# Head norm of the mLSTM inside its output stage, per head and 512 tokens, with the split state in one buffer

## The chip, the cores and the metric

The kernel runs on one core of one Trainium2 chip. The metric is the device time of one execution in microseconds (us), as the median of several runs. Engines are named as the profile names them: PE is TensorE, DVE is VectorE, ACT is ScalarE, POOL is GpSimd, and SP is SyncE, whose queue issues nearly all DMAs.

## What is computed

One encoder layer over two sequences of 1,024 ("prompt") and 2,048 tokens ("sample"), each with 16 learned tokens in front. A single input projection (1,024 to 6,672 columns) feeds two branches: a 2-D neighbourhood attention and a bidirectional mLSTM with four heads of 128. Both go through a final stage with two gates and an output projection. The change is in the end of the mLSTM branch:

```python
h = (h_f + h_b)[:, :, P:].transpose(0, 2, 1, 3)
h = sigmoid(o_pre).reshape(B, L, ML_HEADS, ML_HEAD_DIM) * h
mu = mean(h, axis=-1); var = mean(square(h - mu), axis=-1)
h = (h - mu) * rsqrt(var + EPS)
yb_in = h.reshape(B, L, ML_WIDTH) * head_g          # per-channel gain
yb = (yb_in * silu(ml_z)) @ w_b
```

So each token's 128 values of each head are gated, brought to mean 0 and variance 1, and multiplied by a gain and by a second gate.

## The kernel before

All large products are made in three: an fp32 operand is split into a high and a low part (`xh`/`xl`, `whi`/`wlo`, `cch`/`ccl` and so on), and high x high, high x low and low x high are added in PSUM (`mm3`, L141).

TensorE's order is written by hand; a scheduler orders the instructions of the other engines and the DMAs on SP. TensorE's order comes from two generators. `dense` makes the input projection in groups of 1,024 tokens and, for every 512 tokens, a final block (`final`, `("f", s, b)` in `PLAN`). `sparse` makes, after each other, mLSTM of the prompt, attention of the prompt, mLSTM of the sample, attention of the sample. `run` (L1453) interleaves them: whenever `sparse` yields a cost (`A_A` for a piece of mLSTM outputs, `A_N` for a piece of the norm, in us), `dense` goes on until it has issued that much of its own products. A larger cost therefore puts more dense products between two pieces.

`ml(s)` (L863) works in three stages. For each head `ml_states` goes over the blocks of 256 tokens from the end and keeps the states; `ml_outputs` (L990) goes forward, block by block. One block `b` of `ml_outputs` has six pieces, with a `yield A_A` after each: scores of `b`; first half of the products of `p = b - 1` (`back(p, 0)`); loads; second half (`back(p, 1)`); splits and `finish(p)`; `state(b + 1)`. `state` (L1050) copies the state of a block into its high and low part `cch`, `ccl`, in two buffers, one block ahead of use; `kv` (L1030) does the same for v (`vh`, `vl`). `finish` (L1101) divides by the denominator and stores the block of h, 256 tokens x 128, into the DRAM tensor `H`.

When all heads are done, `ml_norm` (L1158) reads `H` back in blocks of 128 tokens x 4 heads (`hn`), with the gates `tog` (from `TO`) and `szg` (from `SZ`). For each two blocks VectorE gates, takes mean and variance (`bn_stats`, `bn_aggr`) and an inverse root in eleven small steps (`rsqrt8`, L125); then it normalises and multiplies by `szg`; TensorE transposes (L1207), ScalarE evicts into `ybo`, and four stores go to `YB`. The pieces of the norm cost `A_N` each. The gain `head_g` is multiplied into `SZ` already when it is made (`tm_store`, L438).

After `ml_norm` of the prompt, `na(0, ...)` (L554) begins: its first loads, `qr` and `kr` (L552), lead to the first scores (L668).

Of the kernel before, what the change touches and what calls it, by code (L numbers as in the profile page):

```python
# [9 lines left out]
F32 = mybir.dt.float32  # L10
# [97 lines left out]
A_NA, A_D, A_A, A_N, A_G = 1.12, 1.63, 1.63, 1.85, 1.3  # L108


class K:
# [55 lines left out]
    def setup2(self):  # L167
# [10 lines left out]
        nc.vector.tensor_scalar(self.cw[:, 12:24], self.cw[:, 12:24], S_K, None, op0=ALU.mult)  # L178
        self.ones = cp.tile([P, P], F32, name="ones")
# [9 lines left out]
        self.H = [t(f"h{s}", [SEQLEN[s], 512]) for s in range(2)]  # L189
# [197 lines left out]
    def tm_unit(self, col, halves, wd):  # L387
# [4 lines left out]
        if C_MZ <= col < C_MO:  # L392
            hg = wp.tile([P, 1, 256], F32, name="hgb", bufs=1)
            nc.sync.dma_start(hg[:, 0, :], _bc(self.i["head_g"], col - C_MZ, wd))
            nc.vector.tensor_scalar(hg, hg, -0.125, None, op0=ALU.mult)
            self.hgt = hg
# [29 lines left out]
    def tm_store(self, col, wd, s, n, cnt, tok, st):  # L426
# [6 lines left out]
        if C_MZ <= col < C_MO:  # L433
# [3 lines left out]
            for a in range(2):  # L437
                nc.vector.tensor_tensor(st[:, a, :wd], st[:, a, :wd], self.hgt[:, 0, :], op=ALU.mult)  # L438
# [551 lines left out]
    def ml_outputs(self, mp, s, h, g, NB, sts):  # L990
# [3 lines left out]
        raws, kfs, vas, ums, convs, qs, kss, vs, shs, cs, nums = ({} for _ in range(11))  # L994

        def load(b):
            if b < NB:
# [32 lines left out]
        def kv(b):  # L1030
            if b < NB:
                kf, va = kfs.pop(b), vas.pop(b)
# [4 lines left out]
                vh = mp.tile([P, CB, 130], F32R, name="vh", bufs=2)  # L1037
                vl = mp.tile([P, CB, 130], F32R, name="vl", bufs=2)
                nc.scalar.activation(f2(vh), f2(va), AF.Copy)
                nc.vector.tensor_tensor(f2(vl), f2(va), f2(vh).bitcast(F32), op=ALU.subtract)  # L1040
                kss[b], vs[b] = (kh, kl), (vh, vl)
# [8 lines left out]
        def state(b):  # L1050

            if b < NB:
                for j in range(CB):
# [5 lines left out]
                cch = mp.tile([P, CB, 260], F32R, name="cch", bufs=2)  # L1059
                ccl = mp.tile([P, CB, 260], F32R, name="ccl", bufs=2)  # L1060
# [22 lines left out]
        def back(b, j):  # L1083
# [12 lines left out]
            if j == 0:  # L1096
                nums[b] = mp.tile([P, CB, 2, 130], F32, name="num", bufs=1)
            num = nums[b]
            nc.vector.tensor_tensor(num[:, j].rearrange("p d c -> p (d c)"), pa[:, :260], tt.rearrange("p d c -> p (d c)"), op=ALU.add)

        def finish(b):  # L1101
# [8 lines left out]
            hb = mp.tile([P, CB, P], F32, name="hb", bufs=2)  # L1110
            for j in range(CB):
                nc.scalar.activation(hb[:, j], num[:, j, 0, 0:P], AF.Copy, scale=den[:, j, 0:1])
                nc.vector.scalar_tensor_tensor(hb[:, j], num[:, j, 1, 0:P], den[:, j, 1:2], hb[:, j], op0=ALU.mult, op1=ALU.add)
            nc.sync.dma_start(self.H[s][t0:t0 + BL, h * P:(h + 1) * P].rearrange("(c p) f -> p c f", p=P), hb)
# [14 lines left out]
        state(0)  # L1129
        yield A_A  # L1130
        for b in range(NB + 1):
            p = b - 1
            if b < NB:
                scores(b)
                conv_a(b + 1)
# [19 lines left out]
            state(b + 1)  # L1155
            yield A_A

    def ml_norm(self, mp, s):  # L1158

        nc = self.nc  # L1160
        N = SEQLEN[s] // (2 * P)
        ld, hs, rr = {}, {}, {}

        def load(i):
            if i < N:
                ld[i] = []
                for e in range(2):
                    rows = slice((2 * i + e) * P, (2 * i + e + 1) * P)
                    hb = mp.tile([P, 4, P], F32, name="hn", bufs=6)
                    to = mp.tile([P, 4, P], F32, name="tog", bufs=4)  # L1170
                    sz = mp.tile([P, 4, P], F32, name="szg", bufs=4)
                    for x, dr in ((hb, self.H), (to, self.TO), (sz, self.SZ)):
                        nc.sync.dma_start(x.rearrange("p a b -> p (a b)"), dr[s][rows, :])
                    ld[i].append((hb, to, sz))

        def stats(i):
            bs = mp.tile([P, 2, 4, 6], F32, name="bs", bufs=2)
            mv = mp.tile([P, 2, 4, 2], F32, name="mv", bufs=2)
            for e in range(2):
                hb, to, _ = ld[i][e]  # L1180
                nc.vector.scalar_tensor_tensor(hb, to, 1.0, hb, op0=ALU.add, op1=ALU.mult)
                for h in range(4):
                    nc.vector.bn_stats(bs[:, e, h], hb[:, h])
                for h in range(4):
                    nc.vector.bn_aggr(mv[:, e, h], bs[:, e, h])
                yield A_N
            ve = mp.tile([P, 2, 4], F32, name="ve", bufs=2)
            nc.vector.tensor_scalar(ve, mv[:, :, :, 1], 4.0 * EPS, None, op0=ALU.add)
            rr[i] = mv, self.rsqrt8(mp, ve, [P, 2, 4])

        def norm(i, e):
            mv, r = rr[i]
            hb, _, sz = ld[i][e]
            for h in range(4):
                nc.vector.tensor_scalar(hb[:, h], hb[:, h], mv[:, e, h, 0:1], r[:, e, h:h + 1], op0=ALU.subtract, op1=ALU.mult)
            nc.vector.tensor_tensor(hb, hb, sz, op=ALU.mult)

        def turn(i, e):
            if i < 0:
                return  # L1200
            hb = ld[i][e][0]
            if e == 0:
                rr[i] = mp.tile([P, 4, 2, P], F32, name="ybo", bufs=2)
            yo = rr[i]
            pt = self.psum("tr", [P, 4, P])
            for h in range(4):
                nc.tensor.transpose(pt[:, h, :], hb[:, h], self.ident)  # L1207
            nc.scalar.activation(yo[:, :, e, :], pt, AF.Copy)
            if e:
                for h in range(4):  # L1210
                    nc.sync.dma_start(self.YB[s][h][:, 2 * P * i:2 * P * (i + 1)], yo[:, h].rearrange("p a b -> p (a b)"))
                ld.pop(i)
                rr.pop(i)

        load(0)
        yield A_N
        for i in range(N + 1):
            if i < N:
                load(i + 1)
                yield from stats(i)  # L1220
                yield A_N
            turn(i - 1, 0)
            if i < N:
                norm(i, 0)
            yield A_N
            turn(i - 1, 1)
            if i < N:
                norm(i, 1)
            yield A_N
        self.done.add(("ml", s))  # L1230
# [283 lines left out]
```

## Time and profile before

| | us |
|---|---|
| median of 3 runs | 2914.11 |
| lowest and highest | 2910.47, 2915.75 |
| the profiled execution itself | 2923.43 |
| its span in the profile | 2921.6 |
| PE busy in the span | 2818.3 |
| DVE busy | 1742.9 |
| ACT busy | 1289.8 |

The profile shows one execution. Busy time is the time in which at least one instruction of the engine runs; matmuls overlap, so that a busy PE still need not be at its fastest. Idle time stands behind the last bar of a group's line, with what ended most of it. `PEclk` is the share of TensorE's full clock that was granted. A stage is read best from busy time in a window (start and end in us from the span's beginning).

### The profile page before, as it was taken

The numbers are of one execution on the slowest core, as the hardware profiler recorded it, in microseconds if no ns is written. First come the engines' busy times: TensorE is split into PE (matmuls) and PEld (weight loads), VectorE is DVE, ScalarE is ACT, GpSimd is POOL, SyncE is SP. The second block draws the span as 40 slices with busy tenths as digits, with TensorE's granted clock in tenths as the row PEclk, the third lists the DMA queues.
The fourth block names the chain that finished last, engine by engine and source line by source line (L and its number), as shares of the span: only waits on it lengthen the run. The fifth ranks groups of instructions, "written<-read, shape, count | busy, mean of one in ns | idle before, by whom it ended". The sixth has DMA issues, their size and how long they took to land.

```text
span 2921.6 us, 49506 instructions
## 1 busy us (share of the span) xinstructions
PE 2818.3 (96%) x17488; PEld 2511.0 (86%) x17488; DVE 1742.9 (60%) x4722; ACT 1289.8 (44%) x3114; POOL 23.2 (1%) x107
## 2 busy tenths in 40 slices
PE   6999999999799999999999999999999999989998
PEld 6998897899689988788887988888888888879887
DVE  5233566556656665466568776565555557777853
ACT  4112555543244444356566554513444445545421
POOL 1000000000000000000000000000000000000000
PEclk9999999999999999999999999999999999999999
DMA  9655676755875654478679898568669659887975
GB/s 351 220 175 185 201 219 216 270 180 172 294 222 160 205 168 144 143 242 297 202 232 347 279 328 284 157 233 275 199 183 291 206 163 273 249 284 250 295 258 196
DMA packets 438760, 675.26 MB, mean 231 GB/s; under 512 B 52240, under 2 KB 253024, under 8 KB 438512
## 3 DMA queue, kind: packets, MB, share of 16 engines
q1 hardware_dynamic: 437392, 669.41, 70.2%
q0 software_dynamic: 1120, 2.69, 0.4%
q8 instruction: 138, 2.26, 0.3%
q14 instruction: 110, 0.90, 0.1%
HBM read 455.05 MB, written 216.90 MB: 230 GB/s over the span
## 4 chain that ended last, share of the span: by engine, by line
PE 80%; DMA 9%; DVE 7%; issue 2%; ACT 1%; SPq 1%; DVEq 0%; ACTq 0%
PE pj L144 13%; PE pj L145 13%; PE pj L146 13%; PE pj L412 6%; PE pj L413 6%; PE pj L414 6%; PE pj L1326 3%; PE pj L1328 3%; PE pj L1327 3%; PE sm L705 3%; PE tr L693 2%; DMA tg<-gt 2%; DMA um<-ud 1%; PE sc L668 1%; PE sc L669 1%
## 5 line engine op out<-in xcount | busy, mean ns | idle before, releaser
L144 PE MATMUL pj<-xh,whi 128*128 128x512 f32 (+1 forms) x1824 | 720.0, 395 | 0.0
L145 PE MATMUL pj<-xl,whi 128*128 128x512 f32 (+1 forms) x1824 | 702.6, 385 | 0.1
L146 PE MATMUL pj<-xh,wlo 128*128 128x512 f32 (+1 forms) x1824 | 700.9, 384 | 0.0
L412 PE MATMUL pj<-whi,xh 128*128 128x256 f32 (+3 forms) x1576 | 450.0, 286 | 0.0
L413 PE MATMUL pj<-wlo,xh 128*128 128x256 f32 (+3 forms) x1576 | 443.9, 282 | 0.0
L414 PE MATMUL pj<-whi,xl 128*128 128x256 f32 (+3 forms) x1576 | 443.5, 281 | 0.0
L146 PEld LDWEIGHTS pj<-xh,wlo 128*128 128x128 f32 x1824 | 345.4, 189 | 72.3
L144 PEld LDWEIGHTS pj<-xh,whi 128*128 128x128 f32 x1824 | 345.7, 190 | 56.6
L145 PEld LDWEIGHTS pj<-xl,whi 128*128 128x128 f32 x1824 | 346.2, 190 | 54.9 <-DVE xl L310 0.4
L412 PEld LDWEIGHTS pj<-whi,xh 128*128 128x128 f32 (+1 forms) x1576 | 293.5, 186 | 1.2
L413 PEld LDWEIGHTS pj<-wlo,xh 128*128 128x128 f32 (+1 forms) x1576 | 293.2, 186 | 1.1
L414 PEld LDWEIGHTS pj<-whi,xl 128*128 128x128 f32 (+1 forms) x1576 | 293.3, 186 | 0.9
L676 ACT ACTIVATE prb<-sc,mx 128x384 f32<-128x384 f32 (+2 forms) x192 | 120.1, 626 | 237.3 <-DVE mx L672 229.6
L1326 PE MATMUL pj<-whi,mh 128*128 128x256 f32 x768 | 221.1, 288 | 1.1 <-ACT mh L1308 0.7
L1328 PE MATMUL pj<-whi,mlo 128*128 128x256 f32 x768 | 217.7, 284 | 1.8 <-DVE mlo L1309 1.8
L1327 PE MATMUL pj<-wlo,mh 128*128 128x256 f32 x768 | 217.6, 283 | 0.0
L696 DVE TENSOR_TENSOR pts<-tr,pts 96x512 fp32r<-96x512 f32 (+2 forms) x192 | 132.0, 687 | 117.2 <-ACT pts L695 115.9
L421 DVE TENSOR_TENSOR stT<-pj,bb 128x256 f32<-128x256 f32 (+3 forms) x197 | 83.3, 423 | 151.2 <-PE pj L414 147.1
L144 PE MATMUL pj<-yh,whi 128*128 128x512 f32 x384 | 157.4, 410 | 9.3 <-DVE tg L1305 9.3
L695 ACT ACTIVATE pts<-tr 96x512 fp32r<-96x512 f32 (+2 forms) x192 | 114.1, 594 | 115.9 <-PE tr L693 115.6
L672 DVE CUSTOM_DVE_ANT_1 sc<-sc,gt 128x384 f32<-128x384 f32 (+2 forms) x192 | 118.6, 618 | 74.5 <-PE sc L669 62.6
L145 PE MATMUL pj<-yl,whi 128*128 128x512 f32 x384 | 152.8, 398 | 0.0
(234 smaller groups left out, 5069.4 us busy)
## 6 DMA issues: line engine op xcount, KB each, us to landing
whi<-wh SPq DMA_DIRECT2D x176, 512.0 KB
wlo<-wl SPq DMA_DIRECT2D x176, 512.0 KB
wh<-whi SPq DMA_DIRECT2D x64, 512.0 KB
wl<-wlo SPq DMA_DIRECT2D x64, 512.0 KB
wraw<-w_in SPq DMA_DIRECT2D x48, 512.0 KB
gt<-st SPq DMA_DIRECT2D x96, 256.0 KB
tg<-gt SPq DMA_DIRECT2D x96, 256.0 KB
xh<-xh SPq DMA_DIRECT2D x6, 2048.0 KB
```

What stands on the lines that cost most here:

```text
L144: mm(out, ah, bh, start=start, stop=False)
L145: mm(out, ah, bl, start=False, stop=False)
L146: mm(out, al, bh, start=False, stop=stop)
L412: nc.tensor.matmul(o, xh, wh, start=k == 0, stop=False)
L413: nc.tensor.matmul(o, xh, wl, start=False, stop=False)
L414: nc.tensor.matmul(o, xl, wh, start=False, stop=k == KT - 1)
L672: nc.vector.tensor_tensor_reduce(out=so, in0=so, in1=gt[:, g0:g0 + ns, c0:c0 + 32], op0=ALU.add, op1=ALU.min, scale=-1.0, scalar=3.0e38, a ...
L676: nc.scalar.activation(pr_[:, :N].rearrange("p (b a c) -> p b a c", b=4, c=8), sc[:, :N].rearrange("p (a b c) -> p b a c", b=4, c=8), AF.E ...
L696: nc.vector.tensor_tensor(pts[:ks, :, 1, :], pt[:ks], pts[:ks, :, 0, :].bitcast(F32), op=ALU.subtract)
L1326: nc.tensor.matmul(o, mh[:, k, xs], wh, start=k == 0, stop=False)
L1327: nc.tensor.matmul(o, mh[:, k, xs], wl, start=False, stop=False)
L1328: nc.tensor.matmul(o, ml[:, k, xs], wh, start=False, stop=k == KT - 1)
```

## The change

The norm of one head and 512 tokens becomes a generator of its own, `ml_norm(mp, s, h, q, hb, tz)`, made by `finish` when two blocks of `hb` are ready, and stepped by `ml`: one step after each piece of `ml_outputs` and of the next head's `ml_states`. Its first step gates and takes the statistics, the second makes the inverse root, the third normalises and multiplies by `szg`; eight steps later come the four transposes, ScalarE's eviction in place, now with the gain as a scale for each partition, and one store to `YB`. h stays in SBUF; `H` is gone. The gates are loaded by `gates(p)` as 512 tokens x 128 columns. `vh`, `vl`, `cch` and `ccl` have one buffer each; `state(b)` makes all four, at the end of block `b`'s pieces, just before the next block's. `num` takes the place of `tt`. `A_A` is 1.87 instead of 1.63.

```diff
-A_NA, A_D, A_A, A_N, A_G = 1.12, 1.63, 1.63, 1.85, 1.3
+A_NA, A_D, A_A, A_G = 1.12, 1.63, 1.87, 1.3
...
+        self.hg = cp.tile([P, 4], F32, name="hg")
+        nc.sync.dma_start(self.hg, i["head_g"].rearrange("(h p) -> p h", p=P))
+        nc.vector.tensor_scalar(self.hg, self.hg, -0.125, None, op0=ALU.mult)
...
-        self.H = [t(f"h{s}", [SEQLEN[s], 512]) for s in range(2)]
...
-            for a in range(2):
-                nc.vector.tensor_tensor(st[:, a, :wd], st[:, a, :wd], self.hgt[:, 0, :], op=ALU.mult)
...
+                norm = iter(())
                 for h in range(4):
                     sts = {}
-                    yield from self.ml_states(mp, s, h, g, NB, sts)
-                    yield from self.ml_outputs(mp, s, h, g, NB, sts)
-        with tc.tile_pool(name=f"mn{s}", bufs=1, side="right", reuse_waits="tile") as mp:
-            yield from self.ml_norm(mp, s)
+                    for cost in self.ml_states(mp, s, h, g, NB, sts):
+                        next(norm, None)
+                        yield cost
+                    norms = deque()
+                    for cost in self.ml_outputs(mp, s, h, g, NB, sts, norms):
+                        if next(norm, "end") == "end" and norms:
+                            norm = norms.popleft()
+                        yield cost
+                    if norms:
+                        for _ in norm:
+                            pass
+                        norm = norms.popleft()
+                for _ in norm:
+                    yield A_A
+        self.done.add(("ml", s))
...
+        def gates(b):
+            if b % 2:
+                tzs[b // 2] = [mp.tile([P, 4, P], F32, name=n, tag="tz", bufs=2) for n in ("tog", "szg")]
+                for x, d in zip(tzs[b // 2], (self.TO, self.SZ)):
+                    nc.sync.dma_start(x, d[s][(b - 1) * BL:(b + 1) * BL, h * P:(h + 1) * P].rearrange("(c p) f -> p c f", p=P))
...
-                vh = mp.tile([P, CB, 130], F32R, name="vh", bufs=2)
-                vl = mp.tile([P, CB, 130], F32R, name="vl", bufs=2)
-                nc.scalar.activation(f2(vh), f2(va), AF.Copy)
-                nc.vector.tensor_tensor(f2(vl), f2(va), f2(vh).bitcast(F32), op=ALU.subtract)
...
         def state(b):
             if b < NB:
+                va = vas.pop(b)
+                vh = mp.tile([P, CB, 130], F32R, name="vh", bufs=1)
+                vl = mp.tile([P, CB, 130], F32R, name="vl", bufs=1)
+                nc.scalar.activation(f2(vh), f2(va), AF.Copy)
+                nc.vector.tensor_tensor(f2(vl), f2(va), f2(vh).bitcast(F32), op=ALU.subtract)
...
-                cch = mp.tile([P, CB, 260], F32R, name="cch", bufs=2)
-                ccl = mp.tile([P, CB, 260], F32R, name="ccl", bufs=2)
+                cch = mp.tile([P, CB, 260], F32R, name="cch", bufs=1)
+                ccl = mp.tile([P, CB, 260], F32R, name="ccl", bufs=1)
...
-            tt = mp.tile([P, 2, 130], F32, name="tt", bufs=1)
+            if j == 0:
+                nums[b] = mp.tile([P, CB, 2, 130], F32, name="num", bufs=1)
+            num = nums[b]
             for d in range(2):
-                nc.scalar.activation(tt[:, d], pi[:, 130 * d:130 * d + 130], AF.Copy, scale=g[d]["e"][:, cc, h:h + 1])
+                nc.scalar.activation(num[:, j, d], pi[:, 130 * d:130 * d + 130], AF.Copy, scale=g[d]["e"][:, cc, h:h + 1])
...
-            nc.sync.dma_start(self.H[s][t0:t0 + BL, h * P:(h + 1) * P].rearrange("(c p) f -> p c f", p=P), hb)
+            if a:
+                norms.append(self.ml_norm(mp, s, h, q, hbs.pop(q), tzs.pop(q)))
...
-        state(0)
         yield A_A
         for b in range(NB + 1):
             p = b - 1
+            if p >= 0:
+                gates(p)
...
-            state(b + 1)
+            state(b)
...
-    def ml_norm(self, mp, s):
...
+    def ml_norm(self, mp, s, h, q, hb, tz):
+        nc = self.nc
+        to, sz = tz
+        nc.vector.scalar_tensor_tensor(hb, to, 1.0, hb, op0=ALU.add, op1=ALU.mult)
+        bs = mp.tile([P, 4, 6], F32, name="bs", bufs=1)
+        mv = mp.tile([P, 4, 2], F32, name="mv", bufs=1)
+        for j in range(4):
+            nc.vector.bn_stats(bs[:, j], hb[:, j])
+        for j in range(4):
+            nc.vector.bn_aggr(mv[:, j], bs[:, j])
+        yield
+        nc.vector.tensor_scalar(mv[:, :, 1], mv[:, :, 1], 4.0 * EPS, None, op0=ALU.add)
+        rs = self.rsqrt8(mp, mv[:, :, 1], [P, 4])
+        yield
+        for j in range(4):
+            nc.vector.tensor_scalar(hb[:, j], hb[:, j], mv[:, j, 0:1], rs[:, j:j + 1], op0=ALU.subtract, op1=ALU.mult)
+        nc.vector.tensor_tensor(hb, hb, sz, op=ALU.mult)
+        for _ in range(8):
+            yield
+        pt = self.psum("tr", [P, 4, P])
+        for j in range(4):
+            nc.tensor.transpose(pt[:, j, :], hb[:, j], self.ident)
+        nc.scalar.activation(hb, pt, AF.Copy, scale=self.hg[:, h:h + 1])
+        nc.sync.dma_start(self.YB[s][h][:, 512 * q:512 * q + 512], hb.rearrange("p a b -> p (a b)"))
```

More of the change, by code (lines that the diff above doesn't have):

```diff
@@ L391, in tm_unit @@
         nc.sync.dma_start(bb[:, :wd], _bc(self.i["b_in"], col, wd))
[L392 to L396, printed above, removed]
         todo = []
@@ L988, in ml_states, with ml_outputs @@
             yield A_D
-    def ml_outputs(self, mp, s, h, g, NB, sts):
+    def ml_outputs(self, mp, s, h, g, NB, sts, norms):
         nc = self.nc
         f2 = lambda x: x.rearrange("p c t -> p (c t)")
-        raws, kfs, vas, ums, convs, qs, kss, vs, shs, cs, nums = ({} for _ in range(11))
+        raws, kfs, vas, ums, convs, qs, kss, vs, shs, cs, nums, tzs, hbs = ({} for _ in range(13))
         def load(b):
@@ L1031, in kv @@
             if b < NB:
-                kf, va = kfs.pop(b), vas.pop(b)
+                kf = kfs.pop(b)
                 kh = mp.tile([P, CB, P], F32R, name="kh", tag="kh", bufs=2)
@@ L1052, in state @@
             if b < NB:
+                va = vas.pop(b)
[3 more added lines that the diff above has]
+                nc.vector.tensor_tensor(f2(vl), f2(va), f2(vh).bitcast(F32), op=ALU.subtract)
+                vs[b] = vh, vl
                 for j in range(CB):
@@ L1095, in back @@
                 self.mm3(pa[:, 130 * d:130 * d + 130], sh[:, d, j, :], sl[:, d, j, :], vh[:, j, :], vl[:, j, :])
[L1096 to L1099, printed above, removed]
+            nj = num[:, j].rearrange("p d c -> p (d c)")
+            nc.vector.tensor_tensor(nj, pa[:, :260], nj, op=ALU.add)
         def finish(b):
@@ L1109, in finish @@
             nc.vector.reciprocal(den, den)
-            hb = mp.tile([P, CB, P], F32, name="hb", bufs=2)
+            q, a = b // 2, CB * (b % 2)
+            if not a:
+                hbs[q] = mp.tile([P, 2 * CB, P], F32, name="hb", bufs=2)
+            hb = hbs[q]
             for j in range(CB):
-                nc.scalar.activation(hb[:, j], num[:, j, 0, 0:P], AF.Copy, scale=den[:, j, 0:1])
-                nc.vector.scalar_tensor_tensor(hb[:, j], num[:, j, 1, 0:P], den[:, j, 1:2], hb[:, j], op0=ALU.mult, op1=ALU.add)
-            nc.sync.dma_start(self.H[s][t0:t0 + BL, h * P:(h + 1) * P].rearrange("(c p) f -> p c f", p=P), hb)
+                o = hb[:, a + j]
+                nc.scalar.activation(o, num[:, j, 0, 0:P], AF.Copy, scale=den[:, j, 0:1])
+                nc.vector.scalar_tensor_tensor(o, num[:, j, 1, 0:P], den[:, j, 1:2], o, op0=ALU.mult, op1=ALU.add)
+            if a:
+                norms.append(self.ml_norm(mp, s, h, q, hbs.pop(q), tzs.pop(q)))
             for x in (shs, vs, qs, ums):
@@ L1154, in ml_outputs @@
             decay(b + 1, 1)
-            state(b + 1)
+            state(b)
             yield A_A
-    def ml_norm(self, mp, s):
+    def ml_norm(self, mp, s, h, q, hb, tz):
         nc = self.nc
[L1161 to L1230, printed above, removed]
```

2 lines of the change are left out of this document (1 added, 1 removed).

## Prediction, made before the changed kernel was run

> **What bounds the kernel now.** I read the page's first and fourth parts, then busy time by stage, then the groups by line, then the timeline at the places where TensorE stands still.
>
> ```profile
> span 2921.6 us, 49506 instructions
> PE 2818.3 (96%) x17488; PEld 2511.0 (86%) x17488; DVE 1742.9 (60%) x4722; ACT 1289.8 (44%) x3114; POOL 23.2 (1%) x107
> PE 80%; DMA 9%; DVE 7%; issue 2%; ACT 1%; SPq 1%; DVEq 0%; ACTq 0%
> ```
>
> TensorE is busy for 2818.3 of 2921.6 us and carries 80% of the chain that ended last. The change adds and removes no product: 24 x 4 transposes of the norm stay 24 x 4. So the time can move only through the 103 us in which TensorE stands idle and through the clock that idling costs. The stages, before the change (mLSTM of the prompt; its norm; entry into the prompt's attention; mLSTM outputs of the sample; the same beside the first and the second final block of the prompt; norm of the sample; its attention):
>
> ```profile
> core 0: us, PE busy (x) PEld busy (x) DVE busy (x) ACT busy (x) POOL busy (x), PEclk, DMA share, GB/s
> 340.00:716.00 376.00, 371.12 (x2658) 346.42 (x2658) 217.81 (x604) 179.03 (x470) 5.87 (x29) 1.00 0.61 200
> 716.00:776.00 60.00, 55.35 (x299) 46.33 (x299) 48.08 (x205) 22.96 (x40) 0.00 (x0) 0.97 0.84 289
> 776.00:812.00 36.00, 22.58 (x89) 17.69 (x88) 10.27 (x17) 6.63 (x11) 0.00 (x0) 0.81 0.92 294
> 1288.00:1540.00 252.00, 251.98 (x1291) 211.86 (x1290) 157.66 (x422) 154.19 (x395) 0.70 (x6) 1.00 0.77 253
> 1540.00:1645.00 105.00, 98.61 (x613) 88.31 (x612) 90.01 (x218) 65.27 (x174) 0.30 (x2) 0.97 0.95 329
> 1645.00:1756.00 111.00, 107.30 (x708) 97.67 (x708) 83.03 (x235) 58.53 (x179) 0.20 (x2) 0.98 0.89 303
> 1926.00:2024.00 98.00, 93.34 (x477) 77.72 (x476) 72.62 (x335) 22.95 (x39) 0.25 (x1) 0.98 0.83 282
> 2024.00:2440.00 416.00, 415.06 (x2080) 345.57 (x2079) 225.39 (x549) 196.54 (x414) 1.02 (x2) 1.00 0.70 214
> ```
>
> Each row gives start and end, length, then busy time by engine. Where mLSTM outputs run beside projections alone TensorE is full (251.98 of 252.00); the two norm stages, the entry into the attention and the stretch beside the final blocks are not.
>
> **Part 1: the separate norm stages go.**
>
> ```profile
> L1207 PE MATMUL tr<-ident,hn 128*128 128x128 f32 x96 | 15.4, 285 | 9.3 <-DVE hn L1196 6.0 <-DMA wlo<-wl 1.9 <-issue 1.5
> 760.80 0.66 PE L1207 MATMUL tr<-ident,hn 128*128 128x128 f32 x4 [2.47 <-DVE hn L1196]
> 1948.86 0.63 PE L1207 MATMUL tr<-ident,hn 128*128 128x128 f32 x4 [3.18 <-DVE hn L1196]
> ```
>
> The norm's transposes stand in TensorE's fixed order and waited 9.3 us in total for VectorE's product with the gate. The windows show the same: 60 - 55.35 = 4.65 us idle in the first norm stage, 98 - 93.34 = 4.66 us in the second. The granted clock there is 0.97 and 0.98, which costs another 0.03 x 60 = 1.8 and 0.02 x 98 = 2.0 us. Together 13.1 us.
>
> The Trainium skill, "TensorE: Matmul & The Clock Gate", Part 1, has the clock fall to half only after a whole idle window of about 3.4 us; by that rule neither gap above (2.47 and 3.18 us) would have cost clock and this part would be worth 9.3 us. The windows' 0.97 and 0.98 speak against it, so the clock's 3.8 us stay in.
>
> In the changed program the same transposes come eight pieces after VectorE's last step, each piece holding 1.87 us of dense products by the planner: 15 us of cover for the step below. I take all 13.1 us as gone; bounds 5 (the waits come back singly) and 13.1.
>
> VectorE's cost of one norm, from these rows:
>
> ```profile
> L1181 DVE SCALAR_TENSOR_TENSOR hn<-tog,hn 128x512 f32<-128x512 f32 x24 | 16.3, 687 | 8.4 <-DMA tog<-to 3.9 <-DMA hn<-h 2.9 <-issue 1.4
> L1183 DVE BATCH_NORM_STATS2 bs<-hn 128x6 f32<-128x128 f32 x96 | 21.2, 282 | 0.1
> L1185 DVE BATCH_NORM_AGGREGATE mv<-bs 128x2 f32<-128x6 f32 x96 | 9.7, 161 | 0.0
> L134 DVE TENSOR_TENSOR nwt<-nwt,ve 128x8 f32<-128x8 f32 x36 | 5.7, 162 | 0.3
> L135 DVE SCALAR_TENSOR_TENSOR nwy<-nwt,nwy 128x8 f32<-128x8 f32 (+4 forms) x84 | 15.4, 187 | 1.2
> L1195 DVE TENSOR_SCALAR hn<-hn,mv,nwy 128x128 f32<-128x128 f32 x96 | 25.7, 345 | 0.1
> L1196 DVE TENSOR_TENSOR hn<-hn,szg 128x512 f32<-128x512 f32 x24 | 15.9, 689 | 0.0
> L438 DVE TENSOR_TENSOR stT<-stT,hgb 128x256 f32<-128x256 f32 x48 | 18.2, 421 | 0.5
> ```
>
> One unit of 512 tokens and one head is 0.69 + 4 x 0.28 + 4 x 0.16 + twelve small steps of about 0.18 (2.1) + 4 x 0.35 + 0.69 = 6.6 us. There are 24 such units, as there were 24 blocks of 128 tokens and four heads; but the twelve small steps, shared by two blocks before, now run for each unit: 12 x 2.1 = 25 us more. The gain of the head norm moves into ScalarE's eviction, which takes away the 48 products of L438 (18.2 us busy). VectorE ends about 7 us busier in all, off the path while it is at 60%.
>
> ```profile
> h<-hb SPq DMA_DIRECT2D x48, 128.0 KB
> hn<-h SPq DMA_DIRECT2D x24, 256.0 KB
> ```
>
> DMAs: the 24 loads of `hn`, the 48 stores of `h` (together 12.6 MB) and 24 of 48 `yb` stores go, as do six broadcasts of the gain; the 48 loads of `tog` and `szg` stay, in pieces of 512 bytes a row instead of 2 KB. About 100 issues fewer on SP. That stretches no stage that was bound by issuing, so I cost it at nothing; what hides the gate loads is a lead of four to six pieces.
>
> **Part 2: the entry into the prompt's attention.**
>
> ```profile
> 790.74 0.40 SPq L348 DMA_DIRECT2D mk<-st  x1
> 791.23 0.42 SPq L348 DMA_DIRECT2D mq<-st  x1
> 791.76 1.84 SPq L552 DMA_DIRECT2D qr<-nq  x2
> 793.78 3.21 SPq L552 DMA_DIRECT2D kr<-nk  x2
> 797.76 2.57 SPq L552 DMA_DIRECT2D kr<-nkm  x2
> 804.28 0.69 PE L668 MATMUL sc<-kd,stk 128*128 128x384 f32 x1 [13.12 <-ACT kd L648]
> ```
>
> The first scores wait 13.12 us: the loads of q and k are issued behind the projection's `mk` and `mq` stores, when TensorE is already there. In the changed program's order on SP the same loads stand directly behind the same `mq` store. TensorE, however, meets the first scores later: the prompt's mLSTM has 136 pieces, each with 1.87 instead of 1.63 us of dense work (+32.6), the 23 pieces of 1.85 us of the norm go (-42.6) and nine closing pieces of 1.87 come (+16.8): 7 us more dense products stand ahead, 8 us as counted in the two programs' orders. Loads that start at the same dense position and products that arrive 8 us later leave 13 - 8 = 5 us. I take -8; bounds -13 (all gone) and +5, if SP, held by a weight load, issues them later.
>
> For the sample's mLSTM the sum is 232 x 0.24 + 16.8 - 43 x 1.85 = -7 us, so its attention starts at the same dense position as before, and from there on both programs interleave alike: nothing is booked after 2024 us.
>
> **Part 3: the norm's VectorE work lands inside the output pieces.**
>
> ```profile
> 356.33 0.23 PE L144 MATMUL sc<-qh,kh 128*128 128x128 f32 x1
> 363.05 0.27 PE L146 MATMUL sm<-vh,sl 128*128 128x130 f32 x1
> 368.79 0.22 PE L144 MATMUL sc<-qh,kh 128*128 128x128 f32 x1
> 370.85 0.28 PE L144 MATMUL tr<-cch,qh 128*128 128x260 f32 x1
> ```
>
> One output block takes 368.79 - 356.33 = 12.5 us (six pieces); with six times 0.24 more dense work, 13.9 us. VectorE gains 6.6 / 2 = 3.3 us in each. Beside projections it goes from 157.66 / 252 = 63% to (0.63 x 12.5 + 3.3) / 13.9 = 80%: what the norm stages already had (48.08 / 60 and 72.62 / 98), whose idling came from loads and from tight transposes. I book 2 us there. Beside the prompt's final blocks it is 83.03 / 111 = 75% and comes to (0.75 x 12.5 + 3.3) / 13.9 = 91%. The longer pieces also move more of the final blocks beside outputs: 127 us of dense work instead of 106 by the order, 11 output blocks, 155 us. For its price, the two neighbouring rows: at 75% TensorE idled 3.7 us in 111, at 86% 6.4 us in 105. Carried on to 91%, about 7.5 per 100 us: 11.5 us, against 5 now, and 1.5 us of clock. I book +8; bounds 0 (the waits of these rows are for gate loads, not for VectorE) and +25.
>
> **Part 4: one buffer for the split state and v.** The copies of block b now come after block b-1's last product has read the buffer, instead of a block ahead.
>
> ```profile
> L1061 ACT ACTIVATE cch<-st 128x520 fp32r<-128x520 f32 x48 | 30.5, 636 | 5.5 <-DVE st L1058 4.9
> L1062 DVE TENSOR_TENSOR ccl<-st,cch 128x520 fp32r<-128x520 f32 x48 | 33.4, 695 | 0.2
> L1039 ACT ACTIVATE vh<-va 128x260 fp32r<-128x260 f32 x48 | 20.0, 417 | 14.7 <-DMA va<-mv 14.7
> L1040 DVE TENSOR_TENSOR vl<-va,vh 128x260 fp32r<-128x260 f32 x48 | 20.4, 425 | 8.2 <-ACT vh L1039 8.2
> ```
>
> From the last reader (363.05 + 0.27) to the next user (370.85) are 7.5 us now, about 8.3 with longer pieces. The chain is at most 0.64 + 0.70 + 0.42 + 0.43 = 2.2 us, and the order puts it straight behind the block's last addition. Booked at nothing: three pieces of dense work hide it. Without that cover it is the one-buffer rival below.
>
> **Sum**, on the profiled execution (2923.4 us by itself, span 2921.6): -13.1 - 8 + 2 + 8 = -11, so 2912. The three timed runs have a median of 2914.1, 9.3 below it; the same 11 us from there give 2903.
>
> **Rivals.**
> - More gain: the final stretch costs nothing and the entry's wait goes whole: -13.1 - 13 + 2 = -24, 2890. For it: TensorE idles there for loads of gates. Against: VectorE at 86 to 91% leaves little to catch up with.
> - The entry keeps its wait: -13.1 + 8 + 2 = -3, 2911. For it: issue on SP is held by weight buffers, which the order does not show in time. Against: the 8 us of dense work are there.
> - Slower: bursts on VectorE. One unit's 6.6 us stand in VectorE's queue before evictions of projections; with three banks of 2.8 us each the cover is 8.4 us, and where VectorE is already 3 us late each unit stops TensorE for about 1.2 us. If all 24 do, +29; with the entry unchanged, 2914 - 13 + 29 = 2930. It decides where VectorE's waits for loads stand ahead of the burst; `um` is such a wait:
>
> ```profile
> DVE um L1046 <- DMA um<-ud: 93.6, 52, 5.7
> ```
>
>   Against it: with those 93.6 us of waits TensorE still had 251.98 of 252 us.
> - One buffer: the copies are exposed in each of 48 blocks, 48 x 1.8 = +86 (the chain's 2.2 us less the 0.4 in which ScalarE and VectorE overlap), 2914 - 11 + 86 = 2989. The Trainium skill, "Trainium Kernel Development and Optimization", Best Practices, tells to double-buffer so that transfers and compute overlap, and by it this part loses. The 7.5 us between reader and user speak against it here.
>
> **Chances.** Forecast 0.46; more gain 0.09; entry kept 0.17; bursts 0.22; one buffer 0.06. About 0.2% (6 us) is what a measurement can tell from no change. Faster: forecast, more gain and a few of the entry cases, 0.57; same 0.14; slower: bursts, one buffer and 0.01 of the rest, 0.29. The forecast's own range is 2893 to 2909. The range 2887 to 2930 reaches from the larger gain to the bursts' price and leaves out the one buffer and the tails.
>
> **What would show it.** Right: no idling in front of the norm's transposes; the first attention scores waiting 3 to 8 us instead of 13.12; TensorE idle for 6 to 9 us in each 100 beside the final blocks, with VectorE near 90% busy; no idle before the state's products (`tr<-cch`). Wrong: idle before `pj` products put down to VectorE inside the output blocks, waits of VectorE for `tog` or `szg`, waits on `ccl` or `vl`, or an entry that waits 13 us or more.

## The result, and the profile after

The changed kernel takes 2907.14 us (median of 20 runs, 2897.15 to 2913.49), the kernel before 2915.66 us (median of 20 runs on the same chip, 2908.06 to 2923.41). The ratio is 0.9971 with a 95% interval of 0.9962 to 0.9980: 8.5 us faster, where 11 were forecast. The profiled execution of the changed kernel took 2912.43 us. Single executions of one kernel lie up to 16 us apart, and the profiled one of before (2923.43) lies at the top of its range, so what follows goes by places and not by the difference of two spans.

The page of the changed kernel, its span, busy times and the chain that ended last:

```profile
span 2910.7 us, 49314 instructions
PE 2820.4 (97%) x17488; PEld 2513.6 (86%) x17488; DVE 1749.4 (60%) x4813; ACT 1293.7 (44%) x3114; POOL 23.4 (1%) x107
PE 83%; DMA 9%; DVE 5%; ACT 1%; issue 1%; SPq 0%; DVEq 0%; ACTq 0%
```

TensorE's work is the same, as the count of 17488 products says. VectorE is 6.5 us busier (7 were reckoned). The windows of the same stages, shifted to where they now lie (mLSTM of the prompt; its last pieces, where the norm stage was; entry into the attention; mLSTM outputs of the sample; beside the first final block; beside the second; after it; the last pieces of the sample's mLSTM; its attention):

```profile
core 0: us, PE busy (x) PEld busy (x) DVE busy (x) ACT busy (x) POOL busy (x), PEclk, DMA share, GB/s
340.00:746.00 406.00, 401.70 (x2844) 372.71 (x2843) 255.28 (x792) 190.44 (x489) 5.83 (x28) 1.00 0.61 203
746.00:782.00 36.00, 35.93 (x173) 28.83 (x172) 18.80 (x57) 14.73 (x26) 0.00 (x0) 1.00 0.80 291
782.00:818.00 36.00, 31.38 (x150) 24.92 (x149) 15.76 (x32) 15.84 (x31) 0.00 (x0) 0.95 0.93 303
1288.00:1520.00 232.00, 232.00 (x1176) 194.48 (x1175) 155.00 (x465) 134.60 (x333) 0.60 (x5) 1.00 0.79 261
1520.00:1660.00 140.00, 123.02 (x783) 111.97 (x782) 119.68 (x354) 84.17 (x225) 0.20 (x2) 0.93 0.85 291
1660.00:1722.00 62.00, 58.90 (x322) 49.55 (x321) 49.06 (x121) 23.25 (x65) 0.30 (x2) 1.00 0.99 343
1722.00:1880.00 158.00, 158.00 (x971) 140.10 (x970) 108.09 (x370) 80.88 (x234) 0.20 (x2) 1.00 0.77 256
1880.00:2010.00 130.00, 130.00 (x827) 117.00 (x827) 75.77 (x271) 55.33 (x144) 2.48 (x9) 1.00 0.46 147
2010.00:2420.00 410.00, 409.09 (x2047) 340.10 (x2046) 217.28 (x532) 189.88 (x401) 1.02 (x2) 1.00 0.69 209
```

Where the two norm stages stood, TensorE is full and its clock is 1.00 (35.93 of 36 us; 130.00 of 130). The entry has 31.38 of 36 us instead of 22.58. What is new is the stretch beside the final blocks: 17 us idle in 140, clock 0.93. The groups and the timeline put 12.9 of them in one place:

```profile
L1202 PE MATMUL tr<-ident,hb 128*128 128x128 f32 x96 | 15.2, 283 | 12.9 <-DVE hb L1197 12.9
1572.00 1.09 PE L1202 MATMUL tr<-ident,hb 128*128 128x128 f32 x4 [12.93 <-DVE hb L1197]
794.44 0.44 PE L663 MATMUL sc<-kd,stk 128*128 128x384 f32 x1 [2.04 <-ACT kd L643]
L1184 DVE SCALAR_TENSOR_TENSOR hb<-tog,hb 128x512 f32<-128x512 f32 x24 | 16.5, 688 | 0.4
```

Of 24 norms, 23 have their transposes met without a wait; one waits 12.93 us, eight pieces behind and all. The third row is the first scores of the prompt's attention (13.12 us of waiting before), the fourth shows that VectorE does not wait for the gates `tog`. VectorE's timeline, from that late norm's first step to its last:

```profile
1545.63 0.69 DVE L1184 SCALAR_TENSOR_TENSOR hb<-tog,hb 128x512 f32<-128x512 f32 x1
...
1548.28 1.21 DVE L238 TENSOR_TENSOR wlo<-wraw,whi 128x1024 fp32r<-128x1024 f32 x1
...
1552.49 0.16 DVE L1192 TENSOR_SCALAR mv<-mv 128x4 f32<-128x4 f32 x1
1552.56 0.69 DVE L1283 TENSOR_TENSOR mlo<-tg,mh 128x512 fp32r<-128x512 f32 x1
...
1554.90 0.17 DVE L130 TENSOR_SCALAR nwy<-mv 128x4 int32<-128x4 int32 x1
1554.97 1.22 DVE L238 TENSOR_TENSOR wlo<-wraw,whi 128x1024 fp32r<-128x1024 f32 x1
...
1557.91 0.17 DVE L131 TENSOR_SCALAR nwy<-nwy 128x4 int32<-128x4 int32 x1
...
1571.17 0.68 DVE L1197 TENSOR_TENSOR hb<-hb,szg 128x512 f32<-128x512 f32 x1
```

Two steps of the inverse root (L130 and L131, 0.17 us each) lie 3.0 us apart: between them stand a weight split (`wlo`), a convolution and gate products of the final block. Each small step waits its turn in VectorE's queue, so a norm of 6.6 us of work takes 1571.85 - 1545.63 = 26.2 us there. VectorE has no gap in that time: a window from the first step to the last shows it busy for 26.22 of 26.22 us. The eight pieces were over before.

**Lost time by stretch.** To compare many runs I worked out one figure from all traces: the time from each product's start to the next one's, less the first quartile of that time for products of the same kind over all kernels here. It holds idling and clock together. The rest sums to 2730.8 us in every kernel, so differences between kernels are all in this table (us; one execution each; the headings give the stretches in us from the span's start; before 270 and from 1400 to 1500 the kernels differ little and are left out). The last columns count the dense products not yet issued at two places: at the first product of the sample's gates with the tile `ones` ("left at sample"), and behind the last transpose of the sample's attention (`tr<-ident,prb`, "left at end"). Counted at the very first gate product the numbers are slightly other: 7314 before, 7272 in the changed kernel.

| kernel | 270-1000 | 1000-1400 | 1500-1740 | 1740-2450 | 2450 on | left at sample | left at end |
|---|---|---|---|---|---|---|---|
| before | 54.8 | 17.5 | 25.2 | 18.2 | 33.7 | 7308 | 696 |
| before, one buffer (e2) | 52.2 | 21.1 | 18.4 | 18.3 | 28.0 | 7308 | 696 |
| changed | 34.7 | 24.4 | 35.4 | 14.0 | 29.1 | 7260 | 696 |
| changed again (e5) | 34.5 | 23.2 | 33.3 | 13.7 | 27.4 | 7260 | 696 |
| e1 | 40.8 | 21.6 | 16.9 | 20.6 | 32.2 | 7248 | 636 |
| e6 | 47.2 | 20.5 | 21.3 | 17.9 | 30.2 | 7248 | 696 |
| e4 | 40.7 | 19.5 | 36.8 | 15.5 | 24.0 | 7422 | 900 |
| e7 | 46.4 | 16.5 | 22.1 | 13.3 | 30.4 | 7308 | 696 |
| e9 | 44.6 | 15.1 | 33.9 | 12.6 | 19.1 | 7308 | 768 |
| e10 | 38.0 | 24.6 | 30.2 | 13.3 | 45.5 | 7260 | 636 |
| e8 | 33.9 | 23.8 | 22.4 | 12.5 | 32.2 | 7248 | 684 |
| e12 | 35.0 | 23.4 | 27.9 | 15.4 | 39.1 | 7248 | 624 |
| e11 | 37.5 | 22.2 | 21.8 | 14.2 | 28.5 | 7260 | 696 |

The means of the first two rows against those of the next two: norm of the prompt and entry -18.9, start of the sample's mLSTM +4.5, final blocks +12.6, rest of the mLSTM with its norm -4.4, end -2.6; about -9, as the timing says.

### The profile page after: what moved, and what is told of

Its sections match the earlier page's. It is cut to its first block, busy times and chain, and to the rows that moved or that the text cites. A ratio compares the mean times of both kernels' runs of the same rounds, so it can differ in the third digit from the quotient of the medians.

```text
span 2910.7 us, 49314 instructions
## 1 busy us (share of the span) xinstructions
PE 2820.4 (97%) x17488; PEld 2513.6 (86%) x17488; DVE 1749.4 (60%) x4813; ACT 1293.7 (44%) x3114; POOL 23.4 (1%) x107
## 4 chain that ended last, share of the span: by engine, by line
PE 83%; DMA 9%; DVE 5%; ACT 1%; issue 1%; SPq 0%; DVEq 0%; ACTq 0%
PE pj L144 14%; PE pj L145 14%; PE pj L146 14%; PE pj L409 6%; PE pj L410 6%; PE pj L411 6%; PE sm L700 3%; PE pj L1302 3%; PE pj L1300 3%; PE pj L1301 3%; PE tr L688 3%; PE sc L663 1%; PE sc L664 1%; DMA tg<-gt 1%; PE sm L146 1%
## 5 line engine op out<-in xcount | busy, mean ns | idle before, releaser
L706 DVE TENSOR_TENSOR yg<-sm,yg 64x128 f32<-64x128 f32 x384 | 108.3, 282 | 77.7 <-ACT yg L704 70.1
```

## The experiments

Runs e1 to e4, e5 to e8 and e9 to e12 each shared a chip; every ratio is to the kernel before on that chip. My first theory was that of the prediction: norm stages and entry each give, the final blocks take. The rival: the entry's wait is worth nothing.

**e1, more dense products ahead of the entry, nothing else changed** (before, four pieces of 1.85 us behind the prompt's norm):

```diff
+        if s == 0:
+            for _ in range(4):
+                yield A_N
```

> The kernel before, with four more pieces of 1.85 us of dense products after the prompt's norm and nothing else. Theory (the entry is a matter of alignment: the loads stay at their dense position, the first attention scores come 7.4 us of dense work later): the wait in front of the first scores falls from 13.1 us to about 5, time 2915 - 8 = 2907. Rival (the loads move along with the scores, and the changed kernel's shorter wait has another cause): the wait stays at 11 to 13 us and the time at 2915.

2910.79 us, ratio 1.0005 (0.9993 to 1.0017). In the timeline the wait at the entry is 3.29 us instead of 13.12, but near the end a new one stands:

```profile
2804.51 0.79 PE L144 MATMUL pj<-yh,whi 128*128 128x512 f32 x1 [5.65 <-ACT yh L1246]
```

The last output projection waits for its input. The seven dense microseconds drawn forward are missing there (636 products left instead of 696).

**e2, one buffer for state and v, alone** (before, with the changed kernel's `state(b)`, `bufs=1` for `vh`, `vl`, `cch`, `ccl`).

> The kernel before with only the part on the state: one buffer for vh, vl, cch and ccl, made at the end of the block's own pieces. Theory (7.5 us between the last reader and the next user hide a chain of 2.2 us): no wait of TensorE on the state's products, time within 4 us of 2915. Rival (one buffer exposes the copies): 1.8 us in each of 48 blocks, 2915 + 86 = 3001.

2909.93 us, ratio 1.001 (0.9996 to 1.0023). The group of the state's split and of the product that reads it:

```profile
L1064 DVE TENSOR_TENSOR ccl<-st,cch 128x520 fp32r<-128x520 f32 x48 | 33.3, 694 | 0.1
L145 PE MATMUL tr<-ccl,qh 128*128 128x260 f32 x96 | 27.3, 284 | 2.7 <-DVE ccl L1064 2.7
```

2.7 us of waits in 48 blocks, and 2.2 us more in front of the products that read `vl`, where the rival priced 86.

**e3, VectorE relieved by GpSimd** (changed kernel; the low parts of the final blocks' weights are subtracted on GpSimd):

```diff
-eng = nc.vector if self.nu > 4 else nc.gpsimd
+eng = nc.vector if self.nu > 4 and key[0] == "i" else nc.gpsimd
```

> The changed kernel with the low parts of the final blocks' weights (16 splits of 1.22 us, all beside the prompt's first final block) made by GpSimd instead of VectorE. Theory (the single wait of 12.9 us in front of a norm's transposes at 1559 us is VectorE having more work than time there): with 19 us less on VectorE the wait falls to 3 us or less, time 2907 - 10 = 2897. Rival (VectorE was late because loads of weights and gates came late): the wait stays near 13 us, time 2907 or more, since GpSimd takes 2.3 us for a split.

2906.86 us, ratio 0.9985 (0.9974 to 0.9996): no gain, perhaps a small loss, though the wait at the late norm fell to 7.40 us. VectorE does not get the time that it is spared, as its timeline shows:

```profile
1543.89 2.82 POOL L238 TENSOR_TENSOR wlo<-wraw,whi 128x1024 fp32r<-128x1024 f32 x1 [7.15 <-DMA wl<-wlo]
1544.36 2.62 DVE L1037 SCALAR_TENSOR_TENSOR cv<-th,cv 128x256 f32<-128x256 f32 x1
...
1565.61 2.42 POOL L238 TENSOR_TENSOR wlo<-wraw,whi 128x1024 fp32r<-128x1024 f32 x1 [3.90 <-ACT whi L235]
1565.73 2.31 DVE L133 SCALAR_TENSOR_TENSOR nwt<-nwy 128x4 f32<-128x4 f32 x1
```

Both VectorE instructions start inside a split on GpSimd and end as it ends (1546.98 against 1546.71; 1568.04 against 1568.03). So this run could not tell the theories apart.

**e4, pieces as short as before** (changed kernel, `A_A` 1.63).

> The changed kernel with pieces of 1.63 us as before instead of 1.87. Theory (the norm's VectorE work needs the longer pieces): VectorE goes from 80% to about 89% beside projections and over 100% beside the final blocks, TensorE waits 10 to 20 us more there, time 2917 to 2927. Rival (the length of the pieces does not matter, only the total of dense work): 2907 within 5 us.

2913.08 us, ratio 1.001 (1.0001 to 1.002), some 10 us over the changed kernel by the ratios. The transposes of two norms now wait:

```profile
1533.00 1.08 PE L1202 MATMUL tr<-ident,hb 128*128 128x128 f32 x4 [5.64 <-DVE hb L1197]
...
1703.84 1.09 PE L1202 MATMUL tr<-ident,hb 128*128 128x128 f32 x4 [11.95 <-ACT um L1058]
```

The second row names `um`, the later of two by 0.1 us: that norm's last step on VectorE ended at 1703.69. The longer pieces are thus part of what hides the norm. That this is all of the 10 us is not shown: by the table 1.4 to 3.5 us more are lost beside the final blocks, and 6 more in 270 to 1000.

**e5, the changed kernel again**, beside e6 to e8.

> The changed kernel once more, as it is, so that it stands on the same chip as the next three. Every theory: 0.997 of the kernel before, within 0.001. If the single wait of 12.9 us in front of a norm's transposes is VectorE's overload beside the first final block, it is there again at the same norm, 8 to 13 us long; if it was an accident of that execution, it is under 2 us.

2905.84 us, ratio 0.9975 (0.9965 to 0.9985). The wait is no accident of one execution:

```profile
1572.23 1.09 PE L1202 MATMUL tr<-ident,hb 128*128 128x128 f32 x4 [13.19 <-DVE hb L1197]
```

**e6, e1 with the end given back** (before, four pieces more behind the prompt's norm; the sample's output pieces shorter by what that takes):

```diff
+cost = A_A - 0.032 * s     # each yield of ml_outputs
...
+        if s == 0:
+            for _ in range(4):
+                yield A_N
```

> The kernel before with four more pieces of 1.85 us after the prompt's norm, as in the first run, but with the sample's output pieces shortened by 0.032 us each (232 x 0.032 = 7.4 us), so that the sample's attention and the end stand where they stood. Theory (the first run's gain at the entry, 13 to 3.5 us, was lost at the end, where the last store of the attention came too late for the last final block): entry wait 3 to 5 us, no wait over 4 us in the last 120 us, time 8 to 10 us under the kernel before (0.997). Rival (the entry's wait is no cost, what is behind it absorbs it): 0.9995 to 1.001 as in the first run.

2912.74 us, ratio 1.000 (0.999 to 1.0009). The entry waits 3.88 us, 696 products are left for the end, and still nothing is gained: my theory's 8 to 10 us missed, the rival held.

**e7, the changed kernel with the entry undone** (the prompt's closing pieces shorter by 0.82 us each, the sample's pieces longer by 0.032):

```diff
-                    yield A_A
+                    yield A_A if s else A_A - 0.82
...
+cost = A_A + 0.032 * s     # each yield of ml_outputs
```

> The changed kernel with the entry put back: the nine closing pieces of the prompt 0.82 us shorter each (7.4 us less dense work ahead of its attention), and the sample's output pieces 0.032 us longer each. Theory: the first attention scores wait 10 to 13 us again, and the time is 8 to 10 us over the changed kernel's, so level with the kernel before (0.999 to 1.001): norm stalls gained, final block lost. Rival (the gain of the change is the norm's, not the entry's): within 3 us of the changed kernel, 0.996 to 0.998.

2898.37 us, ratio 0.9955 (0.994 to 0.997), 7.5 us below e5, although the entry waits again:

```profile
796.80 0.69 PE L663 MATMUL sc<-kd,stk 128*128 128x384 f32 x1 [10.45 <-ACT kd L643]
...
1533.13 0.63 PE L1203 MATMUL tr<-ident,hb 128*128 128x128 f32 x4 [2.75 <-DVE hb L1198]
1570.55 1.08 PE L1203 MATMUL tr<-ident,hb 128*128 128x128 f32 x4 [9.25 <-DVE hb L1198]
```

At the three places that I counted, dense products stand here as in the kernel before (4476 done at the first scores of the prompt, 7308 and 696 left as in the table). With these alike, the change is worth 0.45% or 13 us, the price of the two norm stages in the prediction. The stretch beside the final blocks loses 22.1 us here, no more than before (25.2 and 18.4), although two norms wait 12.0 us in it. The windows of that stretch, first in the changed kernel, then here:

```profile
1500.00:1740.00 240.00, 219.92 (x1359) 196.41 (x1358) 199.39 (x574) 130.16 (x352) 0.70 (x6) 0.96 0.90 308
1500.00:1740.00 240.00, 228.00 (x1457) 206.24 (x1456) 207.55 (x599) 138.73 (x379) 0.70 (x6) 0.98 0.92 321
```

In e7 the two norms are all of TensorE's idling (240 - 228.00 = 12.0 us); in the changed kernel it idles 20.1 us, 7.2 of them in front of other products, and the clock is lower.

**e8, transposes sixteen pieces behind** (changed kernel; several norms in flight, three buffers of `hb`, statistics in the gate's tile; the closing pieces scaled so that their sum stays):

```diff
-        for _ in range(8):
+        for _ in range(16):
...
-                hbs[q] = mp.tile([P, 2 * CB, P], F32, name="hb", bufs=2)
+                hbs[q] = mp.tile([P, 2 * CB, P], F32, name="hb", bufs=3)
```

> The changed kernel with the norm's transposes sixteen pieces behind instead of eight: a third buffer of hb, two norms may be under way, the statistics written into the read gate's buffer, the closing pieces shortened to the same total of dense work. Theory (VectorE is only late in one place, and the transposes stand too close behind): the wait of 12.9 us goes (under 2 us), and its clock loss; time 10 to 15 us under the changed kernel, 0.992 to 0.994 of the kernel before. Rival (VectorE full beside the final block stops TensorE elsewhere instead, at evictions): the wait reappears in front of projections or scores and the time stays within 4 us of the changed kernel.

2894.41 us, ratio 0.994 (0.9924 to 0.9955): 11.4 us below e5 and the fastest here; it beats both kernels. All 24 norms together:

```profile
L1204 PE MATMUL tr<-ident,hb 128*128 128x128 f32 x96 | 15.1, 281 | 2.2 <-DVE hb L1199 2.2
```

**e9 and e10, the two halves of e7 singly.**

> The changed kernel with only the prompt's closing output pieces made shorter (1.05 in place of 1.87 each), the sample's pieces left at 1.87. Theory (a short wait at the entry to the prompt's attention brings nothing, and the 8 us that the earlier run gained over the changed kernel came with the entry's order): the entry's wait is back at 9 to 12 us and the time is still near 0.9955 of the kernel before (2898 where it stands at 2912). Rival (the entry's wait is real money, and the 8 us and more came from the sample's pieces of 1.902): the entry waits 9 to 12 us, the wait in front of a norm's transposes near 1560 us stays at 11 to 14 us, and the time is 0.9995 to 1.001 of the kernel before (2911 to 2915).

> The changed kernel with only the sample's output pieces at 1.902 in place of 1.87; the closing pieces of the prompt as in the changed kernel. Theory (the entry's wait brings nothing): the entry waits 1.5 to 4 us and the time is that of the run with both edits, near 0.9955 (2898), or that of the changed kernel, 0.9975 (2905). Rival (the entry's gain of 8 us is real and the longer pieces bring another 12 or more beside the final blocks): both add up, the entry waits 1.5 to 4 us, the wait at the norm near 1560 us is 9 us or less, and the time is 0.992 to 0.9935 (2889 to 2893).

e9: 2900.61 us, 0.996 (0.9946 to 0.9973). e10: 2917.75 us, 1.0015 (1.0002 to 1.0028). The first row is from e9's timeline, the others from e10's:

```profile
797.96 0.69 PE L663 MATMUL sc<-kd,stk 128*128 128x384 f32 x1 [10.78 <-ACT kd L643]
```

```profile
796.06 0.45 PE L663 MATMUL sc<-kd,stk 128*128 128x384 f32 x1 [2.92 <-ACT kd L643]
...
1577.37 1.09 PE L1203 MATMUL tr<-ident,hb 128*128 128x128 f32 x4 [13.20 <-DVE hb L1198]
...
2818.36 0.80 PE L144 MATMUL pj<-yh,whi 128*128 128x512 f32 x1 [6.04 <-ACT yh L1218]
```

The kernel whose entry waits 10.78 us is the faster one, by 17 us: the theory of e9 held. For e10 neither theory had the time. Longer pieces use up dense products during the sample's mLSTM; 636 are left for the end instead of 696, and the last output projection waits, as in e1. In the table e10 loses 45.5 us at the end, e9, with 768 left, 19.1. The edits do not add up; together they leave the 696 of before.

**e11, VectorE relieved without GpSimd** (changed kernel, final weights only):

```diff
+                if key[0] == "i":
+                    ...
+                else:
+                    nc.scalar.activation(lo[:, :n], raw[:, :n], AF.Copy)
```

> The changed kernel with the lo parts of the final blocks' and output projections' weights written by ScalarE as a plain copy, so that VectorE's subtraction is left out there (the values of those lo parts are not the differences: part of the computation is changed). It takes some 1.2 us per part off VectorE and puts nothing on GpSimd. Theory (VectorE's queue beside the first final blocks is what makes one norm 26 us long, and that norm's lateness is what costs 10 to 14 us there): the wait in front of that norm's transposes falls from 12.9 to under 4 us, the norm's VectorE work lasts 15 us or less, and the time is 8 to 14 us under the changed kernel, 0.9925 to 0.995 of the kernel before. Rival (the stretch is held by the waits on loads and by the clock, and VectorE's queue is only where it shows): the wait falls, and the time stays within 3 us of the changed kernel's, 0.9965 to 0.9985.

2897.49 us, ratio 0.9944 (0.9925 to 0.9963), 8 to 9 us below the changed kernel by the ratios. The same norm in the timeline:

```profile
1541.70 0.69 DVE L1187 SCALAR_TENSOR_TENSOR hb<-tog,hb 128x512 f32<-128x512 f32 x1
...
1561.08 0.69 DVE L1200 TENSOR_TENSOR hb<-hb,szg 128x512 f32<-128x512 f32 x1
1561.91 1.09 PE L1205 MATMUL tr<-ident,hb 128*128 128x128 f32 x4 [3.84 <-DVE hb L1200]
```

The norm still takes 20 us, not the 15 or less that I expected, but that is 6 less than 26, and the wait is 3.84 us. Lost time beside the final blocks falls from 35 to 21.8 us; elsewhere the row of the table stays within 4 us of the changed kernel's. Work in VectorE's queue is thus part of what made that norm late.

**e12, e8 with the longer sample pieces.**

> The version with the transposes sixteen pieces behind, three normed tiles and the statistics in the gate tile, now with the sample's output pieces at 1.902 in place of 1.87. Theory (sixteen pieces have already taken away the wait at the late norm, so longer pieces have nothing left to hide there): within 3 us of the version with 1.87, 0.993 to 0.995 of the kernel before (2892 to 2898). Rival (the longer pieces line up better with the loads of the final blocks whatever the norm does): another 5 to 8 us, 0.991 to 0.9925 (2886 to 2890).

2915.57 us, ratio 1.0011 (0.9999 to 1.0023), 20 us over e8 by the ratios. Both theories missed. As in e10, few products (624) are left and the end waits:

```profile
2815.65 0.80 PE L144 MATMUL pj<-yh,whi 128*128 128x512 f32 x1 [6.85 <-ACT yh L1220]
```

That is not all of it: by the table the end accounts for 7 us between e12 and e8, and the final blocks for 5.5.

## Why the prediction was right, and where it was not

The total came out as said: 8.5 us faster for a forecast of 11, inside the range. Its parts did less well.

**Part 1 (norm stages, -13.1): right.** No norm but one waits, and both windows are full at clock 1.00. The clock went from 0.97 and 0.98 to 1.00 when the gaps of 2.47 and 3.18 us went; this agrees with the clock's 3.8 us standing in the sum. e7, with the entry's wait kept and no more lost beside the final blocks than before, gives 13 us (9 to 17 by its interval). No run takes the norm stages alone.

**Part 2 (entry, -8): the wait fell as described, the money was not there.** It went from 13.12 to 2.04 us, further than the 5 forecast. The loads of q start 8.8 us before TensorE gets there (794.44 - 2.04 = 792.40), instead of 0.6 after:

```profile
783.59 1.32 SPq L547 DMA_DIRECT2D qr<-nq  x2
```

The step that failed is the term of -8 with nothing against it: what those dense products were worth elsewhere was put at nothing. I had treated a shift of dense work as free because its sum over the kernel comes out even. But the products are a fixed stock that covers waits wherever they stand. Drawn ahead of the entry, they leave 7260 instead of 7308 at the start of the sample's mLSTM, where the changed kernel loses 23 to 24 us, and e7 and e9, with 7308, 15 to 16.5. The gates there and the first product of the states in the changed kernel, and last the gates in the kernel before:

```profile
1192.40 1.09 PE L751 MATMUL sm<-g_lf,tri 128*128 128x68 f32 x4 [4.57 <-issue]
1239.20 0.39 PE L144 MATMUL sm<-vwh,kth 128*128 128x260 f32 x1 [2.91 <-ACT kth L965]
1204.92 0.63 PE L756 MATMUL sm<-g_lf,tri 128*128 128x68 f32 x4 [4.52 <-issue]
```

In e9 the gates wait 2.05 us, but in the kernel before, with 7308 too, they wait as long as in the changed one; that wait alone does not explain the difference. Against the kernel before, what is new is the second row, and a granted clock of 0.95 in 1140 to 1290, where before and e9 have 0.99. Where the stock is cut at the end instead, the last output projection waits (e1, e10, e12). In e9 the entry keeps its wait and the time is no longer (0.9960 against 0.9975, the intervals overlap), and e6, where the entry's wait is shorter and the end keeps its 696, gains nothing: the net worth of the entry's shorter wait is nothing, or less. Why 48 products fewer cost up to 8 us at the sample's start is not settled; the kernels made from the one before (17.5 and 21.1 with 7308, 20.5 and 21.6 with 7248) show it less clearly.

**Part 3 (VectorE inside the output pieces): mechanism right, sizes off.** Beside projections I booked 2 us and TensorE stayed full (232.00 of 232.00): 0. Beside the final blocks I booked 8; lost time rose by 12.6. Idling came to (140 - 123.02 + 62 - 58.90) / 202 = 9.9 per 100 us, just over the 6 to 9 forecast, with VectorE at (119.68 + 49.06) / 202 = 84% and not 91%. I had carried idling on from VectorE's mean share. It came instead mostly as one wait on one norm, whose small dependent steps each queue behind longer work; in those 26 us VectorE was at 100%. e8 (more lag, with a third buffer of `hb`) and e11 (less work on VectorE) cut it to 2.2 and 3.84 us, and both give 8 to 11 us. How the wait turns into time is only in part clear: in e7 norms wait 12.0 us and the stretch loses no more than before.

**Part 4 (one buffer, 0): right.** e2 shows 1.001, and in the changed kernel's waits the chain hardly appears; `vl` waits on `vh`, which waits for v's load, and TensorE for neither:

```profile
DVE um L1056 <- DMA um<-ud: 73.1, 47, 5.1
DVE tg L1279 <- DMA tg<-gt: 25.2, 15, 4.4
DVE vl L1067 <- ACT vh L1066: 8.7, 7, 2.5
```

The double-buffer rule of the Trainium skill ("Trainium Kernel Development and Optimization", Best Practices) would have had this part lose; with three pieces of other products between reader and next user it cost nothing that e2 can tell from zero (0.9996 to 1.0023).

**Rivals.** "More gain" needed the final blocks to cost nothing; e8 shows that this was to be had (2894) with a longer lag. "The entry keeps its wait" fell as a statement about the wait, though its time, 2911, was as close to 2907 as my 2903. "Bursts on VectorE" named the right engine: 1 norm in 24 stopped TensorE, not all, and `um`'s waits (73.1 us against 93.6 before) were not what decided. That the total came so close owes something to errors of opposite signs. By the table the entry gained more than I booked (18.9 us with the prompt's norm, whose 6.5 I take off: about 12 instead of 8), the final blocks lost 12.6 instead of 8, and the sample's start lost 4.5 that I had not booked at all. Nor do the parts add as separate prices: -13 for the norms, nothing for the entry and +12.6 for the final blocks would leave almost no gain, where 8.5 us were measured. What a part costs changes with the place of the dense products, as e7, e9 and e10 show, so the table tells where one pair of kernels differs, and not what each part would be worth alone.

## What to carry to other kernels

Work that covers waits is a stock: before booking a gain where some of it is moved to, count what is left at each later place that it covered, above all at the end. A chain of small dependent steps on a queue shared with long work takes as many turns as it has steps, so its lag is to be set by the turns (26 us here) and not by its busy time (6.6 us). A mean busy share of an engine (84% here) tells little of the one place where it comes late (100% for 26 us).

## What was unexpected of the hardware

A subtraction on GpSimd over 128 x 1024 elements can hold up VectorE: `cv` (L1037) took 2.62 us under it (first row of VectorE in e3's fence), a step on 128 x 4 elements (L133) 2.31. Of the 16 such subtractions beside the final blocks in e3, 14 hold one VectorE instruction to their end in this way; during the other two (at 1549.92 and 1613.91 us) VectorE runs several instructions at their usual lengths. In the changed kernel's timeline, with the split on VectorE, the same two instructions take 0.42 and 0.16:

```profile
1559.31 0.42 DVE L1037 SCALAR_TENSOR_TENSOR cv<-th,cv 128x256 f32<-128x256 f32 x1
1559.65 0.16 DVE L133 SCALAR_TENSOR_TENSOR nwt<-nwy 128x4 f32<-128x4 f32 x1
```

The Trainium skill, "SBUF — State Buffer", Terms, says of the port pair that the two engines share that it is locked for a whole instruction and that the loser blocks fully; the two rows of e3, which end with the split, agree.
